# A hybrid encoder layer: when the chunk states are computed inside the z projection

## The chip, the core and the metric

The kernel runs on one core of a Trainium2 chip. A core has five engines with queues of their own, each working through its instructions in order: TensorE (PE in the profile, with its weight loads as PEld) for matrix products, VectorE (DVE) and ScalarE (ACT) for elementwise work, GpSimd (POOL) for elementwise work too, and SyncE (SP), which here only issues transfers. They wait for one another by semaphores. The metric is the time of one execution on the device, in microseconds (us), as the median of several runs.

## What is computed

One layer of an encoder over 1024 positions of width 1024, in float32: a token mixer with two parallel branches, cross-attention to a memory of 256 positions, and a squared-ReLU MLP. The change touches only the state-space branch (SSD). Cut to that branch:

```python
h = rmsnorm(x, norm_mix[i])
proj = h @ w_in[i]                      # q, k, v, z, x/B/C, dt, gates
xbc = jax.nn.silu(depthwise_conv_centred(xbc, conv_w, conv_b))
...
CB = einsum('bclgn,bcsgn->bcgls', Cc, Bc)
Wd = CB[:, :, :, None] * segsum_exp(adt)
y_diag = einsum('bcgrls,bcsgrp->bclgrp', Wd, xdt)
states = einsum('bcsgn,bcgrs,bcsgrp->bcgrpn', Bc, decay_states, xdt)
# carry: prev[c + 1] = prev[c] * chunk_decay[c] + states[c]
y_off = einsum('bclgn,bcgrpn,bcgrl->bclgrp', Cc, prev, exp(a_cs))
...
y = (y_fwd + y_bwd + d_skip * xs) * silu(z)    # then a grouped RMSNorm
```

The sequence is cut into 8 chunks of 128 positions. The scan runs forward and backward; both directions share x, B and C. There are 8 groups of 4 heads; each has its own B and C with a state width of 128.

## The kernel before

A product of float32 precision is made of three faster ones: each operand is split into a high part (ACT rounds it) and a low part (the rest), and `mm3` (lines 82 to 90) issues high x high, high x low and low x high. Weights arrive by DMA from SP's queue into `raw`; ACT writes the high part `whi` (L66), POOL the low part `wlo` (L69).

`ssd_phase` (line 416) handles the 8 groups one after another. PE's order is written out by hand: the phase runs under `manual_schedule` for PE. The order of the instructions on the other engines is made by a planner from their dependencies, so that it need not be that of the code. A group is a list of jobs: projections of x (two), C and B channels with the convolution behind each (`conv_job`), a gate projection (`gate_job`), and last the projection to z (`z_job`, line 454). Each job is a generator that yields after every step of its own matmuls; the loop at line 637 counts the steps and, at steps named in a dictionary `at`, issues other work between them. So the smaller products of the scan are dealt in between the long projections: `step` of the group before (the outputs of its chunks, 7 down to 0) in the convolution and gate jobs, the chunk states of the own group in the z job.

The z job has 64 steps, of three matmuls of 256 columns each (L85, L89, L90 into `zp`); every 16 steps a bank of 512 columns is done, and ACT's tanh (L473) and a DVE product (L474) turn it into `zs`. Its dictionary holds, before the change:

- step 4, `tm_b`: eight transposes of B on PE (L482), after which ACT writes the high half `bh` (L484) and DVE the low half `bl` (L486), each in two instructions of four chunks.
- steps 8, 16, ..., 64, `state` of chunks 0 to 7 (lines 502 to 526): DVE makes `xs` (L509), x times the decay; ACT its high part `xh` (L513); POOL its low part `xl` (L514); PE multiplies `bh` x `xh` (L517), `bl` x `xh` (L518) and `bh` x `xl` (L519) into a PSUM bank `st`; DVE scales the forward carry and adds the new state (L523, L524); ACT copies the backward state (L526; L521 for chunk 0). Chunks 0 and 7 have only one direction and half the columns. `xs`, `xh` and `xl` have two buffers each.
- step 56 `prep` of chunk 7, step 64 `prep` of chunk 6 and `mask` of chunk 7. `prep` (line 534) fetches rows of the cumulated decay by two DMAs from ACT's queue, masks them on POOL (L540, L542), and makes `ef` from eight exponentials on ACT (L549, L550) and a DVE addition (L551). The exponentials of chunks 7, 6 and 5 are tied behind the second, third and fourth tanh of z. `mask` (line 553) multiplies C and B on PE (L556) and the result into `ef` on DVE (L558); `step` reads it on PE (L572).

The transposed banks, `zp`, `st`, `cb`, `yo` and `yt` share four PSUM banks (tag `p`). The convolution behind the C projection, which comes just before the z job, is one ACT instruction (L379), four DVE steps over 1024 columns (L383, L385), a tanh on ACT (L387) and a final DVE product (L388).

Of the kernel before, what the change touches and what calls it, by code (L numbers as in the profile page):

```python
# [19 lines left out]
NT = 8  # L20
# [395 lines left out]
def ssd_phase(kx, ins, dr):  # L416
# [4 lines left out]
    with tc.tile_pool(name="p1", bufs=1) as sp, tc.manual_schedule(engines={mybir.EngineType.PE}):  # L421
# [9 lines left out]
        def conv_job(q, i):  # L431
            def load():
                return wload(kx, ins["wssd"][q.g, i])

            def run(w):
                ps = psum_g(kx, "cps")
                yield from fm_chunks(kx, ps, w)
                conv_post(kx, q, i, ps)
            return load, run

        def gate_job(m):
            def load():
                return wload(kx, ins["wg"][m])

            def run(w):
                ps = psum_g(kx, "gps")
                yield from fm_chunks(kx, ps, w)
                gt = ca.tile([P, 2, 512], F32, tag="tab", bufs=2, name="gt")
                for h in range(2):
                    A.activation(gt[:, h], ps[:, h * 512:(h + 1) * 512], AF.Tanh, scale=0.5)  # L450
                    nc.sync.dma_start(dr.gt[m][h], gt[:, h])
            return load, run

        def z_job(q):
            def load():
                zhl = [sp.tile([P, 1024], F32R, tag=f"z{i}", bufs=1, name=f"z{i}") for i in range(2)]
                return [wload(kx, ins["wssd"][q.g, 4], hi=zhl[0], lo=zhl[1]), wload(kx, ins["wssd"][q.g, 5])]

            def run(zw):
                zws = wsplit(zw[0], 4) + wsplit(zw[1], 4)  # L460
                q.zt = []
                q.zs = sp.tile([P, NT, 256], F32, tag="zs", bufs=1, name="zs")
                for b in range(3, -1, -1):
                    zp = kx.pp.tile([P, 512], F32, tag="p", name="zp")
                    for j in range(2):
                        t = 2 * b + j
                        for k in range(NK):
                            mm3(kx, zp[:, j * 256:(j + 1) * 256],
                                act_pair(kx.hT[t // 4], k, slice((t % 4) * P, (t % 4) * P + P)),
                                zws[k], k == 0, k == NK - 1)  # L470
                            yield
                    zb = q.zs[:, 2 * b:2 * b + 2].rearrange("p c q -> p (c q)")
                    q.zt.append(A.activation(zb, zp, AF.Tanh, scale=0.5))  # L473
                    V.scalar_tensor_tensor(zb, zb, 1.0, zp, ALU.add, ALU.mult)  # L474
            return load, run
# [137 lines left out]
        def job(lr, at):  # L613
            jobs.append((lr, at))

        for g in range(NG):
            q, o = gs[g], gs[g - 1]
            scan = lambda *cs: [(step, o, c) for c in cs] if g else []
            if g == 0:
                job(conv_job(q, 3), {8: [(tm_x, q)]})  # L620
            else:
                job(conv_job(q, 0), {8: [(step, o, 7)], 16: [(step, o, 6)]})
                job(conv_job(q, 1), {8: [(step, o, 5)], 16: [(step, o, 4)]})
                job(gate_job(g), {8: [(step, o, 3)], 16: [(step, o, 2)]})
                job(conv_job(q, 2), {8: [(step, o, 1)], 16: [(yt, o), (step, o, 0)]})
                job(conv_job(q, 3), {8: [(tm_x, q)], 16: [(yt, o)]})
            at = {8 * c + 8: [(state, q, c)] for c in range(NT)}
            at[4] = [(tm_b, q)]
            at[56] += [(prep, q, 7)]
            at[64] += [(prep, q, 6), (mask, q, 7)]  # L630
            job(z_job(q), at)
        q = gs[7]
        job(gate_job(8), {6: [(step, q, 7)], 12: [(step, q, 6)]})
# [969 lines left out]
def hybrid_encoder(ctx, tc, ins, out, dbg=None):  # L1603
# [25 lines left out]
    with tc.tile_pool(name="dtc", bufs=1) as dtc:  # L1629
        kx.coef = dtc.tile([P, 2, 4, 2, 32], F32, name="coef")  # L1630
        kx.ebias = dtc.tile([P, 2, 4, 2, 32], F32, name="ebias")
        kx.ecs = dtc.tile([P, 2, 4, 2, 32], F32, name="ecs")
        kx.dec = dtc.tile([P, P, 4], F32, name="dec")
        with tc.tile_pool(name="conv", bufs=1) as kx.conv_pool:
            phase0(kx, ins, dr)
            ssd_phase(kx, ins, dr)
# [89 lines left out]
```

## Time and profile before

| what | value |
|---|---|
| median of 3 runs | 2377.24 us (2377.21 to 2386.31) |
| profiled execution | 2381.32 us |
| its span, first to last instruction | 2379.5 us |
| mean granted TensorE clock | 0.993 |
| ACT busy / POOL busy | 1156.0 us (49%) / 950.0 us (40%) |
| DMA | 251.04 MB, mean 105 GB/s |

The profile records one execution. Its rows have the start or the busy time in us, the engine, the line of the kernel (L518 is line 518) and the tiles written and read (`st<-xh,bl`). In the view of waits a row says which engine and line waited for which, the total in us, how often, and the longest. In the view by windows a row has a stretch of time, its length, then the busy time of each engine with the number of its instructions, the granted share of TensorE's clock, the share of the DMA engines and GB/s. In the order of time a bracket at the end of a row has the idle time of that engine before the instruction and what ended it. Times within the span are counted from its start. Ends of matmuls are modelled, so their starts are the better guide.

In the chain of work that ended last PE has 76% of the span, DVE 11%, ACT 4%.

### The profile page before, as it was taken

The numbers are of one execution on the slowest core, as the hardware profiler recorded it, in microseconds if no ns is written. First come the engines' busy times: TensorE is split into PE (matmuls) and PEld (weight loads), VectorE is DVE, ScalarE is ACT, GpSimd is POOL, SyncE is SP. The second block draws the span as 40 slices with busy tenths as digits, with TensorE's granted clock in tenths as the row PEclk, the third lists the DMA queues.
The fourth block names the chain that finished last, engine by engine and source line by source line (L and its number), as shares of the span: only waits on it lengthen the run. The fifth ranks groups of instructions, "written<-read, shape, count | busy, mean of one in ns | idle before, by whom it ended". The sixth has DMA issues, their size and how long they took to land.

```text
span 2379.5 us, 32503 instructions
## 1 busy us (share of the span) xinstructions
PE 2326.0 (98%) x11876; PEld 1946.9 (82%) x11876; DVE 1617.0 (68%) x2539; ACT 1156.0 (49%) x2462; POOL 950.0 (40%) x891
## 2 busy tenths in 40 slices
PE   9999999999999999999999999999999999999998
PEld 7888888888888888877777888788987887788887
DVE  4767666666766664365668977975686456689984
ACT  4455555555564555386765442345553333234341
POOL 2355646465564645254540013205475444200010
PEclk9999999999999999999999999999999999999999
DMA  6222323232332323111116247202253345722301
GB/s 219 89 76 93 98 72 115 75 103 80 98 89 80 116 67 102 45 36 54 41 49 248 80 159 256 89 1 98 98 173 120 111 137 166 281 102 74 130 27 71
DMA packets 150036, 251.04 MB, mean 105 GB/s; under 512 B 11250, under 2 KB 86130, under 8 KB 149876
## 3 DMA queue, kind: packets, MB, share of 16 engines
q1 hardware_dynamic: 79264, 210.67, 25.9%
q10 hardware_dynamic: 70612, 38.29, 5.8%
q8 instruction: 94, 1.54, 0.3%
q14 instruction: 66, 0.54, 0.1%
HBM read 201.47 MB, written 47.45 MB: 105 GB/s over the span
## 4 chain that ended last, share of the span: by engine, by line
PE 76%; DVE 11%; ACT 4%; issue 3%; DMA 3%; POOL 2%; SPq 0%; ACTq 0%; POOLq 0%; DVEq 0%
PE dps L1496 10%; PE mps L1496 8%; PE pb L1291 5%; PE cps L90 4%; PE cps L85 4%; PE cps L89 4%; PE pc L1291 3%; PE zp L85 2%; PE zp L89 2%; PE zp L90 2%; PE cb L572 2%; PE yo L576 2%; PE gps L85 2%; PE gps L89 2%; PE gps L90 2%
## 5 line engine op out<-in xcount | busy, mean ns | idle before, releaser
L69 POOL TENSOR_TENSOR wlo<-raw,whi 128x1024 fp32r<-128x1024 f32 x104 | 255.0, 2452 | 406.8 <-ACT whi L66 390.0
L1447 ACT ACTIVATE kt<-row 128x512 fp32r<-128x512 f32 x264 | 144.2, 620 | 184.3 <-PE dps L1496 82.9
L1496 PE MATMUL mps<-kt 128*128 128x512 f32 x1008 | 230.6, 390 | 2.4 <-DVE kt L1448 2.4
L1496 PE MATMUL dps<-kt 128*128 128x512 f32 x1008 | 228.6, 389 | 0.0
L1496 PEld LDWEIGHTS mps<-kt 128*128 128x128 f32 x1008 | 188.8, 188 | 43.1 <-DVE kt L1448 4.2
L1496 PEld LDWEIGHTS dps<-kt 128*128 128x128 f32 x1008 | 189.3, 188 | 39.2
L85 PE MATMUL cps<-kt,whi 128*128 128x512 f32 x512 | 215.0, 420 | 0.0
L66 ACT ACTIVATE whi<-raw 128x1024 fp32r<-128x1024 f32 x104 | 109.6, 1055 | 198.3 <-DMA raw<-in_wa_dram 51.7
L90 PE MATMUL cps<-kt,wlo 128*128 128x512 f32 x512 | 200.0, 391 | 0.0
L89 PE MATMUL cps<-kt,whi 128*128 128x512 f32 x512 | 199.3, 389 | 0.0
L1448 DVE TENSOR_TENSOR kt<-row,kt 128x512 fp32r<-128x512 f32 x264 | 172.0, 698 | 3.5 <-ACT kt L1447 3.5
L124 POOL TENSOR_TENSOR rr<-rv,mhalf 128x1 f32<-128x1 f32 (+1 forms) x50 | 35.0, 701 | 236.1 <-DVE rv L122 230.1
L514 POOL TENSOR_TENSOR xl<-xs,xh 128x512 fp32r<-128x512 f32 (+1 forms) x64 | 81.6, 1276 | 112.6 <-ACT xh L513 111.2
L1237 POOL TENSOR_TENSOR wop<-w,wop 128x512 fp32r<-128x512 f32 x64 | 85.8, 1344 | 86.4 <-ACT wop L1236 79.1
L89 PEld LDWEIGHTS cps<-kt,whi 128*128 128x128 f32 x512 | 96.3, 188 | 25.4 <-issue 6.7
L85 PEld LDWEIGHTS cps<-kt,whi 128*128 128x128 f32 x512 | 96.3, 188 | 25.0 <-issue 5.7
L90 PEld LDWEIGHTS cps<-kt,wlo 128*128 128x128 f32 x512 | 96.1, 188 | 20.6
L549 ACT ACTIVATE ef<-rows,ebias 128x128 f32<-128x128 f32 x256 | 90.1, 391 | 41.9 <-PE cb L572 41.7
L550 ACT ACTIVATE eb<-rows,ebias 128x128 f32<-128x128 f32 x256 | 88.7, 392 | 28.1 <-POOL rows L542 28.0
L1176 POOL TENSOR_TENSOR wd<-row,wd 128x1024 fp32r<-128x1024 f32 x4 | 11.2, 2799 | 228.4 <-ACT wd L1175 228.4
L85 PE MATMUL gps<-kt,whi 128*128 128x512 f32 x240 | 102.3, 426 | 0.0
L744 POOL TENSOR_SCALAR t<-t,den 128x384 f32<-128x384 f32 (+1 forms) x128 | 69.2, 560 | 80.4 <-DVE den L742 70.9
(377 smaller groups left out, 6604.6 us busy)
## 6 DMA issues: line engine op xcount, KB each, us to landing
rows<-d_cs ACTq DMA_DIRECT2D x128, 256.0 KB, 3.9
raw<-in_wssd_dram SPq DMA_DIRECT2D x48, 512.0 KB, 3.7
raw<-in_wup_dram SPq DMA_DIRECT2D x40, 512.0 KB, 3.8
d_u<-c SPq DMA_DIRECT2D x64, 256.0 KB, 2.3
row<-in_wdn_dram SPq DMA_DIRECT2D x28, 512.0 KB, 6.4
row<-d_u SPq DMA_DIRECT2D x28, 512.0 KB, 6.6
x<-in_x_dram SPq DMA_DIRECT2D x16, 512.0 KB, 6.7
raw<-in_wg_dram SPq DMA_DIRECT2D x16, 512.0 KB, 3.8
```

The source lines that it names most:

```text
L66: steps = [nc.scalar.activation(hi, raw, AF.Copy)]
L69: steps.append((eng or nc.gpsimd).tensor_tensor(lo, raw, hi.bitcast(F32), ALU.subtract))
L85: i = mm(out, l[0], r[0], start=first, stop=False)
L89: mm(out, l[0], r[1], start=False, stop=False)
L90: mm(out, l[1], r[0], start=False, stop=last)
L549: A.activation(ef[:, h], rows[:, 0, h], AF.Exp, bias=kx.ebias[:, b, j, 0, o:o + 1])
L550: A.activation(eb[:, h], rows[:, 1, h], AF.Exp, bias=kx.ebias[:, b, j, 1, o:o + 1])
L1237: self.kx.nc.gpsimd.tensor_tensor(t[:, 1], src, t[:, 0].bitcast(F32), ALU.subtract)
L1291: self.kx.nc.tensor.matmul(ps, w[:, i, ks], act[:, k, j], start=start and k == 0 and m == 0, stop=k == 3 and m == 2, skip_group_check=True)
L1447: nc.scalar.activation(t[:, j, 0], src, AF.Copy)
L1448: nc.vector.tensor_tensor(t[:, j, 1], src, t[:, j, 0].bitcast(F32), ALU.subtract)
L1496: self.kx.nc.tensor.matmul(ps[t], lt[:, k, x, ts], rt[:, k, y], start=n in (1, 2, 5) and k == 0 and m == 0, stop=k == 3 and m == 2, skip_g ...
```

## The change

The steps of the z job at which the chunk states are issued become later and closer. For groups 1 to 7 the first state moves from step 8 to 17, and the eight states then stand at 17, 23, 30, 36, 43, 49, 56 and 63. For group 0 the first moves from 8 to 21, and they stand at 21, 27, 33, 39, 45, 51, 57 and 63. `tm_b` stays at step 4. `prep` of chunk 7 moves from step 56 to 58; `prep` of chunk 6 and `mask` of chunk 7 stay at 64, without a state before them there. Nothing else changes.

```diff
@@ -624,10 +624,11 @@
                 job(gate_job(g), {8: [(step, o, 3)], 16: [(step, o, 2)]})
                 job(conv_job(q, 2), {8: [(step, o, 1)], 16: [(yt, o), (step, o, 0)]})
                 job(conv_job(q, 3), {8: [(tm_x, q)], 16: [(yt, o)]})
-            at = {8 * c + 8: [(state, q, c)] for c in range(NT)}
+            first = 17 if g else 21
+            at = {first + (63 - first) * c // 7: [(state, q, c)] for c in range(NT)}
             at[4] = [(tm_b, q)]
-            at[56] += [(prep, q, 7)]
-            at[64] += [(prep, q, 6), (mask, q, 7)]
+            at.setdefault(58, []).append((prep, q, 7))
+            at[64] = [(prep, q, 6), (mask, q, 7)]
             job(z_job(q), at)
         q = gs[7]
         job(gate_job(8), {6: [(step, q, 7)], 12: [(step, q, 6)]})
```

## The prediction, made before the changed kernel ran

> **What bounds the kernel now.** I read the page first, then the waits of TensorE, then the eight z stages by window, then the order of time inside one of them.
>
> ```profile
> span 2379.5 us, 32503 instructions
> PE 2326.0 (98%) x11876; PEld 1946.9 (82%) x11876; DVE 1617.0 (68%) x2539; ACT 1156.0 (49%) x2462; POOL 950.0 (40%) x891
> ```
>
> TensorE (PE) is busy for 98% of the span and runs its instructions in the order in which the code writes them. Only three things can therefore shorten the kernel: less PE work (the change has none), less PE idle time, or PE work at a better clock. The waits of PE are short, and one stands out (columns: total us, times, longest us):
>
> ```profile
> PE st L518 <- DVE bl L486: 16.5, 8, 4.0
> PE pb L1291 <- DVE c L1360: 3.2, 2, 1.8
> ```
>
> Eight waits are one in each group: the second matmul of the first chunk state needs `bl`, the low half of B, which VectorE (DVE) writes. The longest took 4.0 us, so the other seven share 12.5, 1.79 each. Next, the eight z stages, from the first to the last z matmul:
>
> ```profile
> core 0: us, PE busy (x) PEld busy (x) DVE busy (x) ACT busy (x) POOL busy (x), PEclk, DMA share, GB/s
> 115.46:150.50 35.04, 31.00 (x224) 30.00 (x223) 23.84 (x30) 16.00 (x38) 14.28 (x13) 0.90 0.15 44
> 223.74:255.87 32.13, 30.33 (x226) 29.33 (x225) 21.71 (x29) 16.36 (x40) 12.42 (x11) 0.95 0.21 66
> 329.11:359.74 30.63, 28.84 (x226) 27.84 (x225) 21.85 (x29) 16.47 (x40) 12.37 (x11) 1.00 0.22 69
> 432.98:465.12 32.14, 30.36 (x226) 29.35 (x225) 21.72 (x29) 16.35 (x40) 12.31 (x11) 0.95 0.22 67
> 538.36:570.47 32.11, 30.33 (x226) 29.33 (x225) 21.85 (x29) 16.36 (x40) 12.36 (x11) 0.95 0.21 66
> 643.71:675.83 32.12, 30.34 (x226) 29.34 (x224) 21.79 (x29) 16.36 (x40) 12.24 (x10) 0.95 0.22 66
> 749.07:779.69 30.62, 28.83 (x226) 27.83 (x224) 21.94 (x29) 16.46 (x40) 12.08 (x10) 1.00 0.23 69
> 852.93:885.07 32.14, 30.36 (x226) 29.36 (x225) 21.71 (x29) 16.35 (x40) 12.48 (x11) 0.95 0.21 65
> ```
>
> The work is equal, the lengths are not. Two groups keep the clock (1.00) and take 30.63; five have 0.95 and take 1.50 more; the first has 0.90. Finer slices show where the clock goes: the slice with group 1's stall, the one after it, and the one after group 2's stall:
>
> ```profile
> 227.60:231.00 3.40, 1.60 (x13) 1.40 (x13) 3.40 (x5) 0.91 (x2) 0.25 (x1) 1.00 0.46 154
> 231.00:234.40 3.40, 3.40 (x18) 3.40 (x17) 3.07 (x4) 0.00 (x0) 1.03 (x1) 0.50 0.00 0
> 336.40:339.80 3.40, 3.40 (x28) 3.27 (x27) 3.40 (x6) 1.41 (x3) 1.23 (x2) 1.00 0.00 0
> ```
>
> In group 1 the slice after the stall runs at half clock, 18 matmuls for group 2's 28. So a stall has two prices: itself, and in six groups of eight a slice of slow matmuls behind it.
>
> **The change part by part.** No instruction is added or removed: PE's order in the z stages changes, and through it when DVE, ScalarE (ACT) and GpSimd (POOL) are asked for their parts. The state step carries one `xs` product, `xh`, `xl`, three matmuls and the additions into `prev`; no DMA goes with it.
>
> First the step's price and the position of `bl` in group 1:
>
> ```profile
> 226.35 0.28 PE L90 MATMUL zp<-whi,kt 128*128 128x256 f32 x1
> 227.42 0.28 PE L90 MATMUL zp<-whi,kt 128*128 128x256 f32 x1
> 227.54 0.28 PE L517 MATMUL st<-xh,bh 128*128 128x256 f32 x1
> 229.62 0.39 PE L518 MATMUL st<-xh,bl 128*128 128x256 f32 x1 [1.80 <-DVE bl L486]
> 224.91 2.87 DVE L509 TENSOR_TENSOR xs<-xtok,coef 128x512 f32<-128x512 f32 x1 [1.18 <-POOL xl L514]
> 227.69 1.27 DVE L383 SCALAR_TENSOR_TENSOR cC<-cps,cols,cC 128x1023 f32<-128x1023 f32 x1
> 228.89 0.67 DVE L486 TENSOR_TENSOR bl<-tm,bh 128x512 fp32r<-128x512 f32 x1
> 229.49 1.27 DVE L385 SCALAR_TENSOR_TENSOR cC<-cps,cols,cC 128x1023 f32<-128x1023 f32 x1
> ```
>
> The two L90 rows are three steps apart: 1.07 us, 0.357 a step. Nine steps are 3.21, so L517 moves from 227.54 to 230.75 and L518 to 230.87. `bl` ends at 229.56, behind a 2.87 us `xs` and one step of the C convolution. Everything ahead of it on DVE was issued before the first state and stays where it is, since `tm_b` stays at step 4: I leave `bl` at 229.56. Margin 1.31 us; the wait goes. Group 0, with 13 steps:
>
> ```profile
> 119.20 0.28 PE L517 MATMUL st<-xh,bh 128*128 128x256 f32 x1
> 123.53 0.58 PE L518 MATMUL st<-xh,bl 128*128 128x256 f32 x1 [4.04 <-DVE bl L486]
> 122.80 0.68 DVE L486 TENSOR_TENSOR bl<-tm,bh 128x512 fp32r<-128x512 f32 x1
> ```
>
> 13 x 0.357 = 4.64: L518 comes to 119.20 + 4.64 + 0.12 = 123.96, `bl` ends at 123.48. Margin 0.48, the smaller one.
>
> What is late next? The remaining states stand closer: 46 steps for seven intervals, six or seven each (six in group 0), where there were eight.
>
> ```profile
> 241.44 0.39 PE L517 MATMUL st<-xh,bh 128*128 128x512 f32 x1
> 245.01 0.39 PE L517 MATMUL st<-xh,bh 128*128 128x512 f32 x1
> 245.86 0.63 ACT L513 ACTIVATE xh<-xs 128x512 fp32r<-128x512 f32 x1 [0.50 <-PE st L518]
> 246.57 1.45 POOL L514 TENSOR_TENSOR xl<-xs,xh 128x512 fp32r<-128x512 f32 x1 [2.43 <-ACT xh L513]
> 239.87 1.52 DVE L523 TENSOR_TENSOR prev<-prev,dec 128x256 f32<-128x256 f32 x1
> 244.52 0.42 DVE L523 TENSOR_TENSOR prev<-prev,dec 128x256 f32<-128x256 f32 x1
> 235.00:240.00 5.00, 5.00 (x40) 4.84 (x39) 4.78 (x8) 2.73 (x6) 1.48 (x2) 1.00 0.00 0
> 240.00:246.00 6.00, 6.00 (x47) 5.73 (x46) 4.38 (x7) 3.87 (x13) 2.41 (x2) 1.00 0.02 4
> ```
>
> An interval now is 3.57 us (241.44 to 245.01): 2.86 of steps and 0.71 of state. Later it is 2.85 (six steps) to 3.21 (seven), in the mean 3.06. `xh` and `xl` have two buffers, so state c waits for L518 of state c-2, then for `xh` and `xl`: from 245.01, `xl` is done at 248.02, 3.0 us, and two intervals are 5.7 at the least. DVE: 9.16 us busy in the 11.00 us from 235 to 246, which hold three and a bit old intervals with four `xs`, so about 2.3 for each `xs` served; under 2.85. Neither chain is at its limit, and I count the closer spacing at nothing; what it costs if DVE loses that room is the second rival.
>
> The moved `prep` of chunk 7 has its two row DMAs on ACT's queue, two POOL selects, eight exponentials and one DVE addition:
>
> ```profile
> 241.64 0.60 ACT L473 ACTIVATE zs<-zp 128x512 f32<-128x512 f32 x1 [1.63 <-PE zp L90]
> 242.66 0.39 ACT L549 ACTIVATE ef<-rows,ebias 128x128 f32<-128x128 f32 x1
> 256.49 0.69 DVE L558 TENSOR_TENSOR ef<-ef,cb 128x512 f32<-128x512 f32 x1 [3.02 <-PE cb L556]
> 261.98 0.45 PE L572 MATMUL cb<-xtok,ef 128*128 128x64 f32 x3
> ```
>
> Its exponentials are tied to the second z tanh (241.64) and run from 242.66, some 10 us ahead of the old step 56; step 58 moves nothing. The mask product still ends (257.18) 4.8 us ahead of its reader at 261.98. The last state comes one step earlier. All at nothing; if ACT's queue did hold the mask up, that 4.8 us is the cover.
>
> **The sum.** Stalls 16.5. Clock: five groups 32.13 - 30.63 = 1.50 each, 7.5; group 0 35.04 - 30.63 - (4.04 - 1.79) = 2.16. Together 26.2 us, leaving 30.63 - 1.79 = 28.84 per z stage. After the z stage PE is bound again by its own work, so the gain reaches the end. The profiled execution took 2381.32 (span 2379.5 and 1.8 around it) and would take 2355.1; the median of the three runs, 2377.24, lies 4.1 lower, and from it the forecast is **2351.0**. About 0.5% (11.9 us) is what a measurement of this kernel can tell from no change.
>
> **The rivals.** (1) *The slow slices don't follow the stalls.* Against it: the half clock begins 1.4 us behind the stall of group 1, and where group 2 kept its clock the stage was shorter. For it: two equal stalls of 1.8 us brought none. If only the stalls go: 2377.2 - 16.5 = 2360.7. [...] Chance 0.08.
>
> (2) *The states wait for DVE.* POOL's `xl` and DVE's L523 now overlap more often. L523 took 0.42 alone and 1.52 beside an `xl`: 1.1 more for each state makes 2.3 into 3.4, against 3.06 offered. 0.34 x 6 states x 8 groups = 16 us given back: 2367. Against it: of the two rows above, the slow one stands in a stretch that had no PE wait. Chance 0.14, a third of it with half the price.
>
> (3) *Slower: `bl` falls back behind the C convolution.* DVE's order is not the code's: four `xs`, one convolution step, then `bl`. With a later reader, the planner of that order may put the other three convolution steps (1.20 start to start: 227.69 to 228.89) and the final product ahead of `bl`:
>
> ```profile
> 237.20 1.21 DVE L388 SCALAR_TENSOR_TENSOR cC<-th,cC 128x1024 f32<-128x1024 f32 x1
> ```
>
> It decides from 1.31 + 1.79 = 3.1 us, the third such step. With all four, 3 x 1.20 + 1.21 = 4.8 us, `bl` ends at 234.4: a stall of 3.5 where 1.79 was, 1.7 x 7 = 12; in group 0 4.3 for 4.04; and the slow slice in the two groups that had none, 3 us: 2377.2 + 15.3 = 2392.5. Against it: nothing that precedes `bl` in the order depends on the first state. Chance 0.06, a third of it within 0.5%.
>
> **How the numbers follow.** Forecast 0.72. Faster by over 0.5%: 0.72 + 0.08 + 0.05 = 0.85; within: 0.09 + 0.02 = 0.11; slower: 0.04. The range goes up to 2364, over rival 1 and the mild half of rival 2, and down to 2346: the three runs shown differ by up to 9 us, and if groups 2 and 6 had slow slices in the median run, 3 us more go.
>
> **What would show it.** Right: the row L518 <- L486 gone from PE's waits; eight z stages of about 28.8 us at clock 1.00; DVE still with one C convolution step ahead of `bl`. Wrong: new rows L517, L518 or L519 <- ACT `xh`, POOL `xl` or DVE; clock under 1.00 in a z stage without a stall; `bl` starting later than some 5.5 us after the z stage's start in groups 1 to 7; L572 waiting for `ef`.

## The result, and the profile after

| | before | after |
|---|---|---|
| median | 2378.49 us (4 runs, 2377.21 to 2386.31) | 2352.31 us (4 runs, 2348.77 to 2358.81) |
| ratio, with its 95% interval | | 0.9886 (0.9854 to 0.9918) |
| profiled execution | 2381.32 us | 2358.81 us |
| its span | 2379.5 us | 2357.0 us |
| mean granted TensorE clock | 0.993 | 0.997 |

The change makes the kernel about 26 us faster, 1.1% (some 20 to 35 us by the interval); 2351.0 was forecast, in a range of 2346 to 2364. The profiled pair differs by 22.5 us; single runs of one kernel lie up to 10 us apart, and the profiled run is the slowest of the four after the change.

The page of the changed kernel begins so. PE still fills 98% of the span; it is busy for 9.8 us less although it runs the same 11876 matmuls, because fewer of them run at half clock, where those of 256 columns start 0.21 us apart (group 1 before, from 231.06) and not 0.12. Its z stages have 3.4 us of half clock; before, they had 23.9 (121.76 to 128.58, and 3.41 each from 230.98, 439.20, 545.01, 650.82 and 859.04).

```profile
span 2357.0 us, 32504 instructions
PE 2316.2 (98%) x11876; PEld 1937.7 (82%) x11876; DVE 1623.7 (69%) x2539; ACT 1155.2 (49%) x2462; POOL 956.8 (41%) x891
```

The view of PE's waits has no row for `bl` any more. Of the matmuls of the states these two rows are left, one wait each:

```profile
PE st L519 <- POOL xl L514: 0.9, 1, 0.9
PE st L517 <- ACT xh L513: 0.6, 1, 0.6
```

The z stages by window, group 0 to group 7, from the first to the last z matmul as before (the columns are those of the earlier table; the clock is third from the end):

```profile
116.00:148.56 32.56, 31.07 (x228) 29.55 (x226) 24.91 (x31) 16.22 (x40) 15.55 (x13) 0.95 0.15 45
221.50:250.36 28.86, 28.86 (x230) 28.06 (x227) 21.89 (x29) 16.65 (x41) 13.54 (x11) 1.00 0.24 74
323.25:352.12 28.87, 28.87 (x230) 28.07 (x228) 22.18 (x29) 16.54 (x41) 12.79 (x10) 1.00 0.22 70
425.01:453.88 28.87, 28.87 (x230) 28.07 (x228) 22.16 (x29) 16.54 (x41) 12.79 (x10) 1.00 0.21 68
...
832.45:861.31 28.86, 28.86 (x230) 28.06 (x228) 22.15 (x29) 16.52 (x41) 12.92 (x10) 1.00 0.22 69
```

Groups 1 to 7 are all alike: 28.87 us, PE busy throughout, full clock. Group 0 is not: 32.56 us, 1.5 us idle, clock 0.95. Seven groups do what was forecast; the first trades its old wait for another.

Why `bl` is in time shows in group 1. DVE's order ahead of `bl` is the old one, as the prediction assumed (one convolution step L383, then L486):

```profile
222.66 2.87 DVE L509 TENSOR_TENSOR xs<-xtok,coef 128x512 f32<-128x512 f32 x1 [1.18 <-POOL xl L514]
225.45 1.27 DVE L383 SCALAR_TENSOR_TENSOR cC<-cps,cols,cC 128x1023 f32<-128x1023 f32 x1
226.65 0.67 DVE L486 TENSOR_TENSOR bl<-tm,bh 128x512 fp32r<-128x512 f32 x1
```

and PE reaches the second matmul of the state 1.31 us after `bl` ends (226.65 + 0.67 = 227.32):

```profile
228.51 0.28 PE L517 MATMUL st<-xh,bh 128*128 128x256 f32 x1
228.63 0.28 PE L518 MATMUL st<-xh,bl 128*128 128x256 f32 x1
```

**Where the time went.** From the first z matmul of group 0 to the last of group 7 the two kernels take (before, then after):

```profile
115.46:885.07 769.61, 753.07 (x4368) 655.86 (x4367) 514.17 (x702) 415.28 (x983) 430.28 (x427) 0.98 0.29 89
```

```profile
116.00:861.31 745.31, 743.76 (x4372) 647.23 (x4370) 520.53 (x703) 414.97 (x985) 437.11 (x426) 1.00 0.30 92
```

That is 24.30 us. Outside of it the profiled run after the change is 1.8 us longer (2357.0 - 745.31 against 2379.5 - 769.61), which makes the 22.5. Within it, from group 0's start to group 1's, 108.28 us became 105.50: 2.8 gained where 6.2 were forecast. From group 1's start to the end, 661.33 became 639.81: 21.5 gained where 20.0 were forecast.

### The profile page after: what moved, and what is told of

Its sections match the earlier page's. It is cut to its first block, busy times and chain, and to the rows that moved or that the text cites. A ratio compares the mean times of both kernels' runs of the same rounds, so it can differ in the third digit from the quotient of the medians.

```text
span 2357.0 us, 32504 instructions
## 1 busy us (share of the span) xinstructions
PE 2316.2 (98%) x11876; PEld 1937.7 (82%) x11876; DVE 1623.7 (69%) x2539; ACT 1155.2 (49%) x2462; POOL 956.8 (41%) x891
## 4 chain that ended last, share of the span: by engine, by line
PE 79%; DVE 9%; DMA 3%; ACT 3%; issue 3%; POOL 2%; SPq 0%; POOLq 0%; ACTq 0%; DVEq 0%
PE dps L1497 10%; PE mps L1497 8%; PE pb L1292 6%; PE cps L90 4%; PE cps L85 4%; PE cps L89 4%; PE pc L1292 3%; PE zp L85 3%; PE zp L90 3%; PE zp L89 3%; PE cb L572 2%; PE yo L576 2%; PE gps L85 2%; PE gps L89 2%; PE gps L90 2%
```

## The experiments

Three questions stood open: which part of the edit brings the gain, why group 0 got a new wait, and whether the clock really hangs on the stalls.

**The delay without the spread.** Only the first states move; the later ones stand at the old steps. The diff is against the changed kernel.

```diff
-            at = {first + (63 - first) * c // 7: [(state, q, c)] for c in range(NT)}
+            at = {max(8 * c + 8, first + 3 * c): [(state, q, c)] for c in range(NT)}
             at[4] = [(tm_b, q)]
-            at.setdefault(58, []).append((prep, q, 7))
-            at[64] = [(prep, q, 6), (mask, q, 7)]
+            at[56] += [(prep, q, 7)]
+            at[64] += [(prep, q, 6), (mask, q, 7)]
```

> Only the first states move (17, 20 and 24, then 32, 40 ... 64; in group 0 21, 24, 27, 32, 40 ...): the delay without the even spread. Theory (all of the gain is the wait for bl and the clock behind it): the row L518 waiting for bl is gone, z stages of groups 1 to 7 about 28.5 us to the last z matmul (the state of chunk 7 comes after it, 0.35), the time within 4 us of the changed kernel, 2348 to 2357. Rival (the spread is needed): chunks 1 and 2 come 3 and 4 steps behind, 1.4 to 2.1 us with the state, where xh and xl take some 2.5 after the state two before, so TensorE waits at L517 or L519 of chunk 2 by some 0.5 us in each group, with no clock loss: 4 us slower than the changed kernel.

Measured: 2356.88 us (ratio 0.9901, 0.9886 to 0.9916), 4.6 us above the changed kernel. That is the rival's figure, and just within the theory's range, but for a reason that neither named. Its z stages of groups 0, 1 and 7:

```profile
115.56:149.69 34.13, 30.78 (x224) 29.12 (x223) 24.01 (x31) 16.11 (x39) 15.11 (x14) 0.95 0.16 47
222.93:251.50 28.57, 28.57 (x226) 27.77 (x225) 21.68 (x29) 16.63 (x40) 13.30 (x10) 1.00 0.23 72
833.77:862.34 28.57, 28.57 (x226) 27.77 (x225) 21.41 (x29) 16.54 (x40) 13.34 (x10) 1.00 0.23 70
```

With the 0.35 us of the last state, which comes behind the last z matmul here, groups 1 to 7 take 28.9, as in the changed kernel. Chunks 1 and 2 follow the first state by three and four steps without a wait, so the rival falls, and the even spread is worth nothing there. Group 0 waits more than in the changed kernel: the view of waits has `st L517 <- ACT xh` with 2.4 us, once. With its last state, its z stage is 1.9 us longer there; the rest of the 4.6 lies within what single runs differ by.

**The spread without the delay.** `first = 8` for all groups, the rest of the change kept.

> The even spread up to step 63 without the delay: first state at step 8 in all groups. Theory: the wait of L518 for bl stays as before the change (16.5 us in all, 4.0 the longest), with the half-clock slices behind most of the stalls: the time of the kernel before, 2372 to 2380, z stages of 30.6 to 32.2 us. Rival (the states' place in the middle and at the end of the stage matters): a part of the 26 us comes with the spread, under 2370.

Measured: 2377.74 us, ratio 0.9995 (0.9986 to 1.0005): no change. The first row of its PE waits is the old one:

```profile
PE st L518 <- DVE bl L486: 16.6, 8, 4.1
```

So the spread brings nothing by itself; the gain comes with the later first state.

**Group 0: one step earlier.** In the changed kernel the new waits of group 0 are those of chunk 2:

```profile
130.70 0.51 PE L517 MATMUL st<-xh,bh 128*128 128x512 f32 x1 [0.62 <-ACT xh L513]
131.05 0.40 PE L518 MATMUL st<-xh,bl 128*128 128x512 f32 x1
132.31 0.51 PE L519 MATMUL st<-xl,bh 128*128 128x512 f32 x1 [0.86 <-POOL xl L514]
```

Here is what ACT did up to then, in order of time:

```profile
122.80 0.60 ACT L473 ACTIVATE zs<-zp 128x512 f32<-128x512 f32 x1 [3.54 <-PE zp L90]
128.80 1.06 ACT L387 ACTIVATE th<-cC 128x1024 f32<-128x1024 f32 x1 [5.40 <-DVE cC L385]
129.77 0.36 ACT L521 ACTIVATE prev<-st 128x256 f32<-128x256 f32 x1
130.03 1.14 ACT L513 ACTIVATE xh<-xs 128x512 fp32r<-128x512 f32 x2
```

ACT is idle for 5.4 us. At the head of its queue stands the tanh of the C convolution (L387), which waits for DVE's last convolution step. Behind it stand the copy of the first state (L521) and `xh` of chunks 2 and 3 (L513), although `xh` of chunk 2 had all it needs when L518 of chunk 0 was done, at about 125.0. In groups 1 to 7, and in group 0 before the change, `xh` of chunk 2 stands ahead of that tanh. In the changed kernel the planner put it behind only in group 0, whose first state is at 21. At 20 the order flips, so that one step tells this theory from one of plain spacing.

```diff
-            first = 17 if g else 21
+            first = 17 if g else 20
```

> Group 0 starts its states at step 20, not 21; all else as changed. One step is 0.36 us of TensorE time. Theory (a queue blocked at its head): with 20 the ScalarE order has xh of chunk 2 ahead of the tanh of the C convolution, with 21 behind it, so the waits of TensorE for xh (0.6) and xl (0.9) in group 0 go and with them the half-clock slice: z stage of group 0 about 28.9 us where the changed kernel has 32.6, a wait for bl of at most 0.2, the median some 3.5 us under 2352.3. Rival (the states stand too close in group 0, intervals of 6 and 7 steps with two buffers): intervals hardly change, the waits for xh and xl stay, 32.2 to 32.6 us.

Measured: 2352.56 us (0.9883, 0.9868 to 0.9898). The half-clock slice (clock 0.95 in group 0's z stage, now 1.00) and the waits for `xh` and `xl` are gone, as the theory says; but the z stage of group 0 takes 30.16 and not 28.9, and the 3.5 us expected don't show in the median (2352.31 in the changed kernel). PE waits 0.23 us for `bl` at chunk 0, and one wait of 0.62 stands elsewhere, at chunk 3:

```profile
133.66 0.50 PE L517 MATMUL st<-xh,bh 128*128 128x512 f32 x1 [0.62 <-ACT prev L526]
```

ACT's order in that run, and below it two rows of DVE:

```profile
125.12 0.63 ACT L513 ACTIVATE xh<-xs 128x512 fp32r<-128x512 f32 x1 [1.55 <-PE st L518]
128.91 1.06 ACT L387 ACTIVATE th<-cC 128x1024 f32<-128x1024 f32 x1 [3.15 <-DVE cC L385]
129.88 0.36 ACT L521 ACTIVATE prev<-st 128x256 f32<-128x256 f32 x1
...
133.22 0.38 ACT L526 ACTIVATE prev<-st 128x256 f32<-128x256 f32 x1 [2.46 <-DVE prev L524]
```

```profile
130.00 1.23 DVE L388 SCALAR_TENSOR_TENSOR cC<-th,cC 128x1024 f32<-128x1024 f32 x1
131.15 1.52 DVE L523 TENSOR_TENSOR prev<-prev,dec 128x256 f32<-128x256 f32 x1
```

Now `xh` of chunk 2 passes, but the copy L521 still stands behind the tanh. It copies the forward state of chunk 0 (not a backward one), with which the carry starts: DVE's L523 of chunk 1 reads what it writes, L524 and L526 come behind that, and PE needs the PSUM bank that L526 frees. On DVE, L523 also stands behind L388, the final product, which needs the tanh; L521 ends at 130.24, but L523 starts at 131.15, when L388 is nearly over. So the tanh holds PE up by a second way, in which DVE's order has a part.

**Group 0: the tanh behind `xh`.** The first state stays at 21; the tanh and final product of the C convolution of group 0 are traced behind the state of chunk 2, with an edge that keeps the tanh behind its `xh`. With it L521 comes ahead of the tanh as well.

```diff
...
+    def tail():
+        th = ca.tile([P, S], F32, tag="tab", bufs=2, name="th")
+        A.activation(th, acc, AF.Tanh)
+        V.scalar_tensor_tensor(acc, th, 1.0, acc, ALU.add, ALU.mult)
+
+    if i == 3 and q.g == 0:
+        q.tail = tail
+    else:
+        tail()
...
+            q.xh = A.activation(xh[:, lo:hi], xf[:, lo:hi], AF.Copy)
...
+        def tail(q):
+            with tc.issue_after(q.xh.ins):
+                q.tail()
...
+            if g == 0:
+                at[first + (63 - first) * 2 // 7].append((tail, q))
```

> As the changed kernel, group 0 at step 21, but in group 0 the tanh and final product of the C convolution are issued behind xh of chunk 2. Theory (queue blocked at its head): no TensorE wait for xh or xl in group 0, clock 1.00 there, z stage 28.9 us, median some 3.5 us under 2352.3. Rival (states too close): the z stage of group 0 stays at 32 or more, since spacing and first step are those of the changed kernel.

Measured: 2351.09 us (0.9875, 0.9859 to 0.9892). Its whole stretch of eight groups, and group 0's z stage:

```profile
117.44:860.06 742.62, 741.62 (x4372) 645.64 (x4370) 517.24 (x702) 414.96 (x984) 438.61 (x426) 1.00 0.30 92
117.44:146.23 28.79, 28.79 (x228) 27.97 (x226) 22.98 (x30) 15.94 (x38) 15.29 (x13) 1.00 0.14 43
```

28.79 with the spacing and first step of the changed kernel: the rival of spacing falls, and the order is shown to be the cause. (L388 moves on DVE with the tanh, so this run alone doesn't part the two queues; in the changed kernel it was ACT's `xh` that PE waited for.) The stretch is 2.7 us shorter than in the changed kernel and 27.0 shorter than before. It is not 3.8 shorter, as the z stage is, because about 1.0 goes again before group 1, with a wait of 0.57 of PE for DVE (`yo` for `t`, L576 and L580 of the other kernels) that the changed kernel doesn't have; why it comes stays open. Of all versions this has the shortest stretch. The 3.5 us expected don't show in the whole times: they don't tell it from the changed kernel, since their intervals overlap.

**Stalls by dose, and the clock.** One kernel has a different first step in each group: 17, 5, 6, 7, 8, 9, 10, 11. From 1.79 us at step 8 and 0.36 a step, the stalls were expected at 2.86, 2.50, 2.15, 1.79, 1.43, 1.07 and 0.72 us in groups 1 to 7, and at 1.25 in group 0, and half clock behind some of those in groups 1 to 4 alone.

```diff
-            first = 17 if g else 21
+            first = 4 + g if g else 17
```

> The first state's step is 17, 5, 6, 7, 8, 9, 10, 11 in groups 0 to 7, the rest spread evenly to 63. [...] Rival (any stall costs clock): a half-clock slice in groups 5 to 7 too.

Measured: 2366.18 us (0.9944, 0.9924 to 0.9964). The second matmul of the first state, groups 1 to 7:

```profile
225.77 0.39 PE L518 MATMUL st<-xh,bl 128*128 128x256 f32 x1 [2.41 <-DVE bl L486]
330.56 0.52 PE L518 MATMUL st<-xh,bl 128*128 128x256 f32 x1 [2.41 <-DVE bl L486]
436.55 0.58 PE L518 MATMUL st<-xh,bl 128*128 128x256 f32 x1 [2.15 <-DVE bl L486]
542.22 0.39 PE L518 MATMUL st<-xh,bl 128*128 128x256 f32 x1 [1.79 <-DVE bl L486]
646.07 0.39 PE L518 MATMUL st<-xh,bl 128*128 128x256 f32 x1 [1.44 <-DVE bl L486]
749.58 0.38 PE L518 MATMUL st<-xh,bl 128*128 128x256 f32 x1 [1.07 <-DVE bl L486]
852.72 0.38 PE L518 MATMUL st<-xh,bl 128*128 128x256 f32 x1 [0.72 <-DVE bl L486]
```

At steps 6 to 11 the stalls are the expected ones to 0.1 us, and from 7 on each step takes off 0.36. At step 5 the stall is 2.41 and not 2.86; another 0.17 goes to `bh`. In group 0, at step 17, PE waits 1.13 us at L517, where 1.25 was expected. The slices that follow the stalls of groups 2, 3 and 4:

```profile
330.60:334.00 3.40, 3.40 (x16) 3.40 (x17) 3.40 (x5) 0.90 (x2) 1.28 (x1) 0.51 0.08 28
436.50:439.90 3.40, 3.35 (x15) 3.35 (x16) 3.40 (x5) 0.90 (x2) 1.29 (x1) 0.50 0.11 43
542.40:545.80 3.40, 3.40 (x27) 3.27 (x28) 3.40 (x5) 0.98 (x3) 1.29 (x1) 1.00 0.02 7
```

Half clock follows the stalls of groups 2 and 3 (2.41 and 2.15 us): 0.51 and 0.50 in the 3.40 us behind them, and 1.00 in those behind group 4's (1.79). From one of the seven rows above to the next it is 104.79, 105.99, 105.67, 103.85, 103.51 and 103.14 us. All seven start when `bl` is there, and from group to group a step less lies between them; with 0.36 a step added back, groups 2 and 3 take some 1.5 us more than groups 1, 4, 5 and 6, which agree within 0.2. So the stalls of 1.44 and 1.07 us brought no half clock, and the rival falls.

Nor does the length alone part the stalls that brought half clock from the others. Group 1's was as long as group 2's (2.41) and brought none. In the kernel before, stalls of 1.77 to 1.80 us brought it in groups 1, 3, 4, 5 and 7, and stalls of 1.79 in groups 2 and 6 did not. In group 0 of the changed kernel two waits of 0.62 and 0.86 us stood ahead of a half-clock stretch (132.89 to 136.30). What decides between them these runs don't show.

**How late is too late.** First steps 21, 12, 13, 14, 24, 30, 36, 42.

```diff
-            first = 17 if g else 21
+            first = (21, 12, 13, 14, 24, 30, 36, 42)[g]
```

> The first state's step is 21, 12, 13, 14, 24, 30, 36, 42 in groups 0 to 7, the rest spread evenly to 63. Theory: the wait for bl is 0.4 at step 12, 0.1 at 13, none from 14, so the delay of 17 has three steps to spare. At the late end the intervals are 2.7, 2.4, 2.1 and 1.8 us; VectorE needs some 2.3 a state, so waits at the states begin at 36 (1 to 2 us in all) and reach 3 to 6 us at 42; at 24 and 30 at most 1 us, if the tanh of the C convolution is ordered ahead of xh or of the copies into prev. Rival (spacing does not matter, only the head of ScalarE's queue): waits of 1 us or less at 36 and 42 as well.

Measured: 2362.43 us in two runs (0.9928, 0.9908 to 0.9948). The stretch of eight groups is only 2.7 us longer than in the changed kernel, the profiled run 2.9; what makes up the rest of the 10 us between the medians stays open. The wait for `bl` is 0.4 at step 12; from 13 on the view of waits has no row for it. The z stages of groups 4 to 7:

```profile
529.17:558.50 29.33, 29.33 (x230) 27.90 (x228) 23.69 (x29) 16.40 (x40) 12.55 (x10) 1.00 0.17 58
631.56:660.38 28.82, 28.82 (x230) 27.99 (x228) 21.76 (x29) 16.45 (x40) 12.24 (x10) 1.00 0.18 59
733.28:762.94 29.66, 29.20 (x230) 28.00 (x228) 23.40 (x29) 16.44 (x39) 13.01 (x10) 1.00 0.19 62
835.84:865.62 29.78, 29.35 (x230) 27.94 (x228) 23.58 (x29) 16.52 (x39) 13.46 (x10) 1.00 0.22 69
```

Waits begin at 36, as expected, but stay at 0.46 and 0.43 us, far less than the 1 to 6 expected: the rival is nearer. (Group 4 is 0.46 longer than 28.87 without a booked wait. The starts of its matmuls show it as gaps of at most 0.14 us at the states of chunks 3 to 6, such as 0.37 from L518 to L519 where 0.23 is usual; what holds them stays open.) Even states 1.8 us apart cost under 1 us a group. There the room is used up, though: in the last 7.2 us of group 7's stage, with some four states, DVE is busy for 6.96, about 1.7 a state. The 2.3 us of the forecast had counted work, the convolution steps above all, that is over before the states close up. In groups 4 to 7 `xh` of chunk 2 stands behind the tanh again, as in group 0, but no wait for it is booked: here the order costs only where the state is due before the tanh is done.

**What makes `bl` late.** The kernel before, with one edge: `xs` of chunk 3 is issued on DVE behind the first half of `bl`.

```diff
+                    i = V.tensor_tensor(low[:, cs], pc, dst[:, cs].bitcast(F32), ALU.subtract)
+                    if b == 0:
+                        kx.bl = i
...
+            with tc.issue_after(kx.bl.ins) if c == 3 else ExitStack():
+                V.tensor_tensor(xf[:, lo:hi].rearrange("p (d h q) -> p d h q", h=4, q=64),
...
```

> The kernel before, states at 8, 16 ... 64, with one edge more: the xs product of chunk 3 is issued on VectorE behind the first half of bl. Theory (bl is late because that xs, 2.87 us beside GpSimd's weight split, stands ahead of it): the wait of L518 falls from 1.79 to about 0.4 us in groups 1 to 7 and from 4.0 to about 1.5 in group 0, no half-clock slice behind it, the time 2353 to 2360: most of the gain of the change without moving a state. Rival (bl is late because of the C convolution step or its input): the wait falls by less than 0.5 us, the time stays above 2370.

Measured: 2357.50 us, ratio 0.9912 (0.9895 to 0.9928). The mean granted clock is 0.999, for 0.993 before. By an estimate that leaves room for no half-clock slice in the eight groups: the traces before and after have 4.99 and 5.48 us of half clock at the end of the span, which alone make 0.999. PE's wait for `bl` (L521 is L518 of the other kernels) is down from 16.5 us to 4.1:

```profile
PE st L521 <- DVE bl L486: 4.1, 8, 1.3
```

In group 1 it is 0.41, in group 0 1.31. Most of the gain is to be had without moving a state: the long `xs` ahead of `bl` made most of the stall. In the changed kernel, too, it takes 2.87 us (the row of 222.66 above) where the one before it takes 0.69, beside POOL's weight split, which starts 0.06 us ahead of it:

```profile
222.60 2.38 POOL L69 TENSOR_TENSOR wlo<-raw,whi 128x1024 fp32r<-128x1024 f32 x1
```

From the start of the one to the end of the other they took 2.93 us, where 2.38 and 0.69 make 3.07. Why the product is long there no run shows.

## Why the prediction was right, point by point

*What bounds the kernel.* Right. PE's idle time and clock were the only things that moved, and no other engine took over.

*The step's price and the margin of `bl`.* Right in groups 1 to 7: margin 1.31 us forecast, 1.31 measured. In group 0 `bl` ends 0.29 us ahead of L518 where 0.48 was forecast; it now gates L517, whose PSUM bank it frees (`bl` ends at 124.42, L517 starts at 124.48), and costs 0.1.

*The closer spacing at nothing.* Right for groups 1 to 7, and the dose runs show room down to states some 1.8 us apart. Wrong for group 0, and this is the step that failed: "Neither chain is at its limit, and I count the closer spacing at nothing". The chain was summed from durations, as if each part ran when its inputs were there. ACT runs in the planner's order, which the later first state had changed, and the tanh L387 stood ahead of `xh`. Cost: waits of 0.62 and 0.86 us and a half-clock slice, which make most of the 3.4 us that the group's gain fell short (2.8 for 6.2). The third rival had the mechanism, a planner that orders anew when a reader comes later, on the wrong queue: it looked at DVE, where the order ahead of `bl` stayed.

*The moved `prep` and mask at nothing.* Right: PE's waits have no row for L572.

*The clock.* Right in groups 1 to 7: 7.5 us of the sum. In five groups it was 0.95 before and is 1.00. The first rival falls by the dose run: of groups 1 to 6 there only 2 and 3 lost clock, behind 2.41 and 2.15 us, and groups 5 and 6, with 1.44 and 1.07, did not. Stalls of 1.77 to 1.80 us brought half clock in five groups of seven before.

*The sum.* 26.2 us forecast and 26.2 between the medians: closer than the argument deserves, since errors cancel and the interval is 15 us wide. The agreement to 0.1 us is luck. Group 0 gave 3.4 less. Groups 1 to 7 gave 1.5 more, because the stalls were priced too low: the view of waits counts idle time from a modelled end of the last matmul. By starts, L517 to L518 took 2.08 in group 1 (227.54 to 229.62) where 0.12 is usual, and L518 to L519 0.22 for 0.12: 2.06 for a stall booked with 1.80. Seven times 0.26 is 1.8; 0.35 goes off, as the last state now stands within the window. The 1.8 us that the profiled run lost outside of the stretch lies within what single runs differ by.

*The second rival.* It fell: nothing of the sort in groups 1 to 7 at 3.1 us, and under 1 us a group at 1.8.

*The third rival.* It fell in groups 1 to 7, and in group 0 `bl` still comes behind one convolution step; what the planner changed was ACT's order.

## What to carry to other kernels

Where one engine has its order written by hand and the others are ordered by a planner, a later reader can reorder every queue behind it: look for an instruction at a queue's head that waits long, with ready work behind it, and hold it back by an edge. A stall of the matrix engine had two prices here, 1.8 us and in five groups of seven 1.5 more: read the clock slice behind it, and price the stall by start to start. Before moving the reader, look at what stands ahead of the writer: one edge on VectorE brought some 21 of the 26 us here.

## What the hardware showed that I had not expected

The granted clock was one half for 3.41 us behind some stalls of PE and stayed full behind others as long: 1.77 to 1.80 us brought half clock in five groups of seven before, and in the dose run 2.15 us and one stall of 2.41 did, while another of 2.41 and one of 1.79 did not. In group 0 of the changed kernel two waits of 0.62 and 0.86 us, 1.6 us from start to start, were followed by it. What decides it these runs don't show.
